# Joined one-hot steps in the expert top-k, and 32 tokens of the second layer on the gathered-row path

## The chip, the core and the metric

The kernel runs on one core of a Trainium2 chip. The metric is the time of one execution on the device in microseconds (us). Engines are named as in the profile: PE is TensorE's matrix multiply and PEld its weight loads, DVE is VectorE, ACT is ScalarE, POOL is GpSimd, SP issues most transfers.

## The reference

The program is a two-layer encoder trunk over 272 tokens (16 learned ones and 256 of the input), model width 1024. Each layer has a token mixer (a recurrent block in layer 0, a convolution module in layer 1) and then an expert layer, the part that matters here:

```python
s1, i1 = lax.top_k(scores[:, :, 0], 16)          # 8 heads, 128 keys on each of two axes
s2, i2 = lax.top_k(scores[:, :, 1], 16)
cand = (s1[..., :, None] + s2[..., None, :]).reshape(c, 8, 256)
s, flat = lax.top_k(cand, 16)
idx1 = jnp.take_along_axis(i1, flat // 16, axis=-1)
idx2 = jnp.take_along_axis(i2, flat % 16, axis=-1)
expert = idx1 * 128 + idx2                       # one of 16384 experts
g = jax.nn.softmax(s, axis=-1)
act = jax.nn.gelu(jnp.einsum('chkd,cd->chk', expert_u[expert], xc))
return jnp.einsum('chk,chkd->cd', g * act, expert_v[expert])
```

Layer 0 computes this for all 272 tokens, layer 1 for 256, since the 16 learned tokens are dropped at the end.

## The kernel before

**Dense path.** For most tokens the kernel doesn't gather experts. It multiplies the tokens with all 16384 rows of U and of V in 128 units each, and masks with the gates. A unit (512 KB) is loaded by SP into `raw`, rounded to fp32r by ACT (`hi`, line 137), and the rest `lo = raw - hi` is made by POOL or DVE (line 144). In U a unit is 24 matmuls: 8 of `hi` with the tokens' high part, 8 of `hi` with their low part, 8 of `lo` with the high part (line 172). Their moving operand has n columns, n the number of dense tokens, 240 in both layers (`LATE[layer][0]`). In V a unit is 8 matmuls of `hi` with both parts side by side (2n = 480 columns, line 632) and 8 of `lo` (240 columns, line 636). Every matmul has its own 128x128 weight load. The last four units of V are split otherwise.

**Top-k and gates.** Ahead of U come the queries (16 units of `w_query`) and the scores (line 522). While the first units of U run on PE, DVE does the top-k of the dense tokens in two tiles of up to 128 partitions (`topk_steps`): per head the best 16 keys of each axis, the 256 sums `cand`, their best 16 (`fi`), and then the key numbers: for each axis the position (`pu`, `pf`) is compared with 0 to 15 (`oh`), multiplied with the axis's key numbers `s16` and added up into `idx`. In this time POOL makes `lo`, two buffers deep; from unit 46 on (`LO_FROM`) DVE makes it, in program order behind all of the top-k. From unit 64 on DVE also builds one-hot gates for 8 tokens at a time, and PE multiplies them (lines 590, 591, 16 matmuls a chunk).

**Gathered-row path.** Groups of 16 tokens (`FEW`), 8 heads each, fill 128 partitions. `few_pick` makes their scores (4 matmul passes) and spreads the token's vector over the heads' rows (16 matmul passes, line 861, with operands that POOL copies, line 859). A top-k of its own gives 16 expert numbers for each row. Then 16 gathers from U by POOL's indirect DMA (line 887) feed 16 dot products on DVE (line 896), and 16 gathers from V feed 16 weighted sums (lines 920, 922); 8 matmuls (16 passes, line 671) add the result to the dense sum. A group in `EARLY` has its top-k ahead of U's unit 46 and 10 of its dot products between units 40 and 63 of U; the rest stands in V. A group in `LATE` has everything in V. Layer 0 has one of each (tokens 256 to 271 early, 240 to 255 late), layer 1 one late group (tokens 240 to 255).

**Order.** The instructions of each engine stand in an order that is fixed when the program is built; `issue_after` ties some of them to others. `few_plan` spreads a layer's gathers, dots and sums evenly over V's units.

Of the kernel before, what the change touches and what calls it, by code (L numbers as in the profile page):

```python
# [17 lines left out]
P = 128  # L18
D = 1024
# [6 lines left out]
NK = 128  # L26
# [5 lines left out]
CC = 8  # L32
HC = 8
FEW = META
EARLY, LATE = ((256,), ()), ((240,), (240,))
DOTS_FROM, DOTS, AHEAD, LO_FROM = 40, 10, 2, 46
JG = 4
JA = 64
# [21 lines left out]
class Trunk:  # L60
# [712 lines left out]
    def topk_steps(self, sp, sc, m, H):  # L773
        nc = self.nc
        K = TOPK
        sv = sp.tile([P, H, 2, K], F32, tag="sv", name="sv", bufs=1)
        si = sp.tile([P, H, 2, K], U32, tag="si", name="si", bufs=1)
        for b in range(2 * H):
            s = sc[:m, b, :]
            v, i = sv[:m, b // 2, b % 2, :], si[:m, b // 2, b % 2, :]  # L780
# [7 lines left out]
        cand = sp.tile([P, H, K, K], F32, tag="cand", name="cand", bufs=1)  # L788
# [3 lines left out]
        fi = sp.tile([P, H, K], U32, tag="fi", name="fi", bufs=1)  # L792
        for h in range(H):
            s = cand[:m, h].rearrange("p a b -> p (a b)")
            v, i = fv[:m, h, :], fi[:m, h, :]
# [4 lines left out]
            nc.vector.max(v[:, 8:16], r[:m])  # L800
            nc.vector.max_index(i[:, 8:16], v[:, 8:16], r[:m])
            yield
        s16 = sp.tile([P, H, 2, K], F16, tag="s16", name="s16", bufs=1)
        nc.vector.tensor_copy(s16[:m], si[:m])
        idx = sp.tile([P, 2, H, K], F32, tag=f"idx{H}", name="idx", bufs=2)
        for ax in range(2):
            pu = sp.tile([P, H, K], U32, tag="pu", name="pu", bufs=1)
            if ax == 0:
                nc.vector.tensor_scalar(pu[:m], fi[:m], 4, None, op0=OP.logical_shift_right)
            else:  # L810
                nc.vector.tensor_scalar(pu[:m], fi[:m], 15, None, op0=OP.bitwise_and)
            pf = sp.tile([P, H, K], F16, tag="pf", name="pf", bufs=1)
            nc.vector.tensor_copy(pf[:m], pu[:m])
            oh = sp.tile([P, H, K, K], F16, tag="oh", name="oh", bufs=1)
            nc.vector.tensor_tensor(oh[:m], self.iota16[:m, None, None, :].to_broadcast([m, H, K, K]),  # L815
                                    pf[:m, :, :, None].to_broadcast([m, H, K, K]), op=OP.is_equal)
            nc.vector.tensor_tensor(oh[:m], oh[:m], s16[:m, :, ax, None, :].to_broadcast([m, H, K, K]), op=OP.mult)  # L817
            nc.vector.tensor_reduce(idx[:m, ax], oh[:m], op=OP.add, axis=AX.X)
            yield
        return idx, fv  # L820

    def softmax(self, sp, fv, m, H=HEADS):
# [17 lines left out]
    def few_pick(self, sp, kp, q, xs, layer, t0):  # L840
# [8 lines left out]
                             start=True, stop=True)  # L849
        sc = (sp if early else kp).tile([P, 2, NK], F32, name=f"sc{t0}", bufs=1)  # L850
        nc.scalar.activation(sc, ps[:, :2], AF.Copy)
        wide = sp.tile([P, D], F32, tag="kept" if early else "rows", name="wide", bufs=1 if early or layer else AHEAD + 1)
        for h in range(2):
            pw = self.bank(5 + h, "wide_ps")
            for lo in range(2):
# [70 lines left out]
    def few_plan(self, vp, kp, early, late, scale, layer, ahead=2):  # L926
        steps = []
        for few in early + late:
            lo = DOTS if few in early else 0
            steps += [lambda few=few: self.few_load(vp, few)]  # L930
            steps += [lambda few=few, lo=lo, k=k: self.few_dot(vp, few, k, lo, TOPK, ahead) for k in range(TOPK - lo + ahead)]
            steps += [lambda few=few: self.few_gelu(few, few is late[-1]), lambda few=few: self.few_weigh(few, scale)]
            steps += [lambda few=few, k=k: self.few_add(vp, few, k, ahead) for k in range(TOPK + ahead)] + [few]
        first = 1 if early else 16
        self.steps = [(first + i * (NK - 4 * JG - first) // len(steps), f) for i, f in enumerate(steps)]
        self.sums = []
        self.picks = [self.few_late(kp, few, layer) for few in late]

# [249 lines left out]
```

## Time and profile before

| | |
|---|---|
| median of 3 executions | 1878.39 us (1878.09 to 1879.69) |
| the profiled execution | 1877.54 us |
| its span, first to last instruction | 1875.7 us, 35733 instructions |
| PE busy | 1809.0 us (96%) |
| PEld busy | 1713.9 us (91%) |
| DVE busy | 1553.2 us (83%) |
| ACT, POOL busy | 943.9 us (50%), 413.8 us (22%) |
| mean granted TensorE clock | 0.990 of 2.4 GHz |

Layer 0's U begins at 189.7 us and its V at 582.6; layer 1's U at 1134.6 and its V at 1514.7. A matmul's duration in the trace holds its passage through the array, so matmuls overlap, and the price of one is the distance from its start to the next one's.

### The profile page before, as it was taken

How to read it: one execution, taken by the hardware profiler on the slowest of the kernel's cores; microseconds unless marked ns; L12 is line 12 of the kernel's file. 1: busy time of each engine (PE TensorE's matmuls, PEld its weight loads, DVE VectorE, ACT ScalarE, POOL GpSimd, SP SyncE). 2: the span in 40 equal slices, each digit the busy share in tenths (PEclk: the TensorE clock that was granted, in tenths of full speed). 3: DMA queues.
4: the chain of work that ended last, by engine and by line, in shares of the span. 5: the costliest groups of instructions: out<-in, count | busy, mean ns of one | idle time of the engine just before them, and what ended most of it. 6: DMA issues, size and time to landing. Idle time of an engine off the chain costs nothing.

```text
span 1875.7 us, 35733 instructions
## 1 busy us (share of the span) xinstructions
PE 1809.0 (96%) x13925; PEld 1713.9 (91%) x13925; DVE 1553.2 (83%) x2793; ACT 943.9 (50%) x1533; POOL 413.8 (22%) x282
## 2 busy tenths in 40 slices
PE   7899998999999999999999999999999999999996
PEld 6789998999998999999899799999999989999995
DVE  8985999889998787777699769996899976776765
ACT  6744543455444444885480545445554445454442
POOL 1111897100001232221000027980000000111200
PEclk9999999999999999999999999999999999999998
DMA  5345566755556898987540355566555567887863
GB/s 200 106 160 167 162 197 181 259 178 161 169 169 231 299 317 274 322 283 267 176 145 25 111 182 162 181 193 196 174 164 168 169 226 233 283 287 254 279 202 112
DMA packets 105337, 376.30 MB, mean 201 GB/s; under 512 B 11600, under 2 KB 12752, under 8 KB 105040
## 3 DMA queue, kind: packets, MB, share of 16 engines
q1 hardware_dynamic: 91344, 323.69, 53.4%
q0 software_dynamic: 13824, 50.34, 8.1%
q8 instruction: 109, 1.79, 0.4%
q14 instruction: 60, 0.49, 0.1%
HBM read 369.20 MB, written 4.78 MB: 199 GB/s over the span
## 4 chain that ended last, share of the span: by engine, by line
PE 78%; DVE 13%; issue 5%; POOL 2%; ACT 1%; DMA 0%; POOLq 0%; SPq 0%; DVEq 0%; ACTq 0%
PE u L172 36%; PE acc L632 22%; PE acc L636 12%; PE cv L1078 2%; PE g L590 1%; PE g L591 1%; DVE lo L144 1%; POOL lo L144 1%; DVE oh L815 1%; DVE oh L817 1%; DVE si L783 1%; DVE r L784 1%; DVE si L786 1%; DVE cand L789 0%; PE sps L522 0%
## 5 line engine op out<-in xcount | busy, mean ns | idle before, releaser
L137 ACT ACTIVATE hi<-raw 128x1024 fp32r<-128x1024 f32 x587 | 620.9, 1059 | 651.9 <-PE u L172 214.7
L144 DVE TENSOR_TENSOR lo<-raw,hi 128x1024 fp32r<-128x1024 f32 x500 | 611.7, 1226 | 216.7 <-PE acc L636 109.6
L172 PE MATMUL u<-xs,hi 128*128 128x240 f32 (+2 forms) x5120 | 656.1, 279 | 15.7 <-ACT xs L206 5.7
L172 PEld LDWEIGHTS u<-xs,hi 128*128 128x128 f32 x5120 | 617.4, 190 | 20.0 <-ACT xs L318 7.1
L632 PE MATMUL acc<-w,hi 128*128 128x480 f32 x1984 | 474.1, 381 | 2.0 <-DVE w L209 2.0
L632 PEld LDWEIGHTS acc<-w,hi 128*128 128x128 f32 x1984 | 354.4, 188 | 47.4 <-DVE w L209 2.4
L172 PE MATMUL u<-xs,lo 128*128 128x240 f32 (+2 forms) x2560 | 357.0, 280 | 16.2 <-DVE lo L144 8.1
L172 PEld LDWEIGHTS u<-xs,lo 128*128 128x128 f32 x2560 | 322.8, 190 | 21.0 <-POOL lo L144 10.5
L636 PEld LDWEIGHTS acc<-w,lo 128*128 128x128 f32 x2048 | 268.0, 189 | 18.2 <-DVE lo L144 3.4
L636 PE MATMUL acc<-w,lo 128*128 128x240 f32 x2048 | 273.4, 275 | 1.3 <-DVE lo L144 1.3
L144 POOL TENSOR_TENSOR lo<-raw,hi 128x1024 fp32r<-128x1024 f32 x92 | 243.2, 2664 | 82.6 <-ACT hi L137 65.0
L887 POOL DMA_INDIRECT rows<-u_rows,ids x48 | 61.8, 1287 | 713.3 <-ACT hi L137 269.9
L887 POOL DMA_INDIRECT rows<-peer_v,ids x48 | 68.9, 1435 | 224.8 <-DVE few_out L922 125.4
L597 ACT ACTIVATE act_b<-g 128x496 f32<-128x496 f32 (+29 forms) x60 | 23.5, 391 | 117.3 <-DVE act_b L560 99.1
L573 DVE TENSOR_TENSOR AB<-iota,iT 128x2048 f16<-128x2048 f16 x60 | 73.0, 1217 | 0.0
L590 PE MATMUL g<-AB 128*128 128x128 f16 x480 | 60.6, 220 | 0.0
L591 PE MATMUL g<-Bl,AB 128*128 128x128 f16 x480 | 60.0, 219 | 0.0
L896 DVE SCALAR_TENSOR_TENSOR rows<-rows,wide 128x1024 f32<-128x1024 f32 x48 | 58.5, 1218 | 0.0
L922 DVE SCALAR_TENSOR_TENSOR few_out<-rows,act,few_out 128x1024 f32<-128x1024 f32 x45 | 57.5, 1279 | 0.0
L316 POOL TENSOR_SCALAR xs<-x,par 128x272 fp32r<-128x272 f32 (+1 forms) x6 | 6.0, 997 | 227.9 <-DVE x L308 165.9
L209 DVE TENSOR_TENSOR w<-act_b,w 128x960 fp32r<-128x960 f32 x32 | 36.9, 1153 | 15.4 <-ACT w L206 15.3
L590 PEld LDWEIGHTS <-AB 128*128 128x128 f16 x480 | 45.4, 97 | 1.9
(256 smaller groups left out, 1713.8 us busy)
## 6 DMA issues: line engine op xcount, KB each, us to landing
raw<-peer_u SPq DMA_DIRECT2D x256, 512.0 KB, 3.9
raw<-peer_v SPq DMA_DIRECT2D x248, 512.0 KB, 4.5
raw<-w_query SPq DMA_DIRECT2D x32, 512.0 KB, 3.6
raw<-pw SPq DMA_DIRECT2D x24, 512.0 KB, 3.6
raw<-w_in SPq DMA_DIRECT2D x16, 512.0 KB, 4.4
raw<-w_out SPq DMA_DIRECT2D x8, 512.0 KB, 4.2
raw<-peer_v SPq DMA_DIRECT2D x16, 256.0 KB, 3.8
wide<-wide SPq DMA_DIRECT2D x6, 512.0 KB, 3.3
```

The lines of the kernel that those rows point to most:

```text
L137: self.act_hi = nc.scalar.activation(hi, raw, AF.Copy).ins
L144: i = e.tensor_tensor(lo[:, s], raw[:, s], hi[:, s].bitcast(F32), op=OP.subtract)
L172: self.mm = nc.tensor.matmul(ps[:, :n], l[:, k, :], xs(k, r)[:, :n], start=start, stop=stop)
L573: nc.vector.tensor_tensor(AB.rearrange("p x c (a b) -> p (x c) a b", b=2), keys, iT[:, c0 // HC].rearrange("p x c b -> p (x c) b")[:, :, N ...
L590: nc.tensor.matmul(ps[:, c, :], A, Bh, start=True, stop=False)
L591: nc.tensor.matmul(ps[:, c, :], A, Bl, start=False, stop=True)
L632: self.mm = nc.tensor.matmul(acc[b][:, :2 * n].rearrange("p (a t) -> p a t", a=2), hi, w[:, :, :n], start=j == 0, stop=j == NK - JG - 1, s ...
L636: self.mm = nc.tensor.matmul(main[b][:, :n], hi if p_ else lo, w[:, i, :n], start=False, stop=j == NK - 1 and not p_, skip_group_check=True)
L887: self.nc.gpsimd.indirect_dma_start(out=t, out_offset=None, in_=table, in_offset=bass.IndirectOffsetOnAxis(ap=few["ids"][:, i, k:k + 1], a ...
L896: self.nc.vector.scalar_tensor_tensor(t, t, 1.0, few["x"], op0=OP.mult, op1=OP.mult, accum_out=few["act"][:, i:i + 1])
L922: nc.vector.scalar_tensor_tensor(few["out"], t, w, few["out"], op0=OP.mult, op1=OP.add)
L1078: self.mm = nc.tensor.matmul(ps[:, :m], diag[i, b, k], h[j][:, s + k:s + k + m], start=(i, j, k) == steps[0], stop=(i, j, k) == steps[-1])
```

## The change

On VectorE, the position, compare and multiply steps of the two axes become one set of instructions over both axes (`s16`, `pu`, `pf`, `oh`, `idx` hold both). `pf` keeps each position twice, so that the compare reads pairs. `oh` takes the buffer of `cand`. In layer 1 tokens 240 to 255 become an early group and tokens 224 to 239 a late one, and n falls from 240 to 224. Layer 0 keeps its groups.

```diff
-EARLY, LATE = ((256,), ()), ((240,), (240,))
+EARLY, LATE = ((256,), (240,)), ((240,), (224,))
...
+        s16 = sp.tile([P, 2, H, K], F16, tag="s16", name="s16", bufs=1)
+        nc.vector.tensor_copy(s16[:m], si[:m].rearrange("p h a k -> p a h k"))
+        pu = sp.tile([P, 2, H * K], U32, tag="pu", name="pu", bufs=1)
+        fp = fi[:m].rearrange("p h k -> p (h k)")
+        nc.vector.tensor_scalar(pu[:m, 0], fp, 4, None, op0=OP.logical_shift_right)
+        nc.vector.tensor_scalar(pu[:m, 1], fp, 15, None, op0=OP.bitwise_and)
+        pf = sp.tile([P, 2 * H * K, 2], F16, tag="pf", name="pf", bufs=1)
+        nc.vector.tensor_copy(pf[:m], pu[:m].rearrange("p a n -> p (a n)")[:, :, None].to_broadcast([m, 2 * H * K, 2]))
+        yield
+        oh = sp.tile([P, 2 * H, K, K], F16, tag="cand", name="oh", bufs=1)
+        pairs = [m, 2 * H * K, K // 2, 2]
+        nc.vector.tensor_tensor(oh[:m].rearrange("p g k (a b) -> p (g k) a b", b=2),
+                                self.iota16[:m].rearrange("p (a b) -> p a b", b=2)[:, None].to_broadcast(pairs),
+                                pf[:m, :, None, :].to_broadcast(pairs), op=OP.is_equal)
+        nc.vector.tensor_tensor(oh[:m], oh[:m],
+                                s16[:m].rearrange("p a h k -> p (a h) k")[:, :, None, :].to_broadcast([m, 2 * H, K, K]),
+                                op=OP.mult)
+        yield
         idx = sp.tile([P, 2, H, K], F32, tag=f"idx{H}", name="idx", bufs=2)
-        for ax in range(2):
-            pu = sp.tile([P, H, K], U32, tag="pu", name="pu", bufs=1)
...
-            nc.vector.tensor_reduce(idx[:m, ax], oh[:m], op=OP.add, axis=AX.X)
-            yield
+        nc.vector.tensor_reduce(idx[:m].rearrange("p a h k -> p (a h) k"), oh[:m], op=OP.add, axis=AX.X)
+        yield
...
-        first = 1 if early else 16
-        self.steps = [(first + i * (NK - 4 * JG - first) // len(steps), f) for i, f in enumerate(steps)]
+        self.steps = [(1 + i * (NK - 4 * JG - 1) // len(steps), f) for i, f in enumerate(steps)]
```

On DVE, at the end of layer 0's top-k (the second tile, 112 tokens), the order before reads:

```order
L809 TENSOR_SCALAR pu<-fi 112x128
L813 CAST pf<-pu 112x128
L815 TENSOR_TENSOR oh<-iota_98,pf 112x2048
L811 TENSOR_SCALAR pu<-fi 112x128
L817 TENSOR_TENSOR oh<-oh,s_2460 112x2048
L813 CAST pf<-pu 112x128
L818 TENSOR_REDUCE idx<-oh 112x128
L815 TENSOR_TENSOR oh<-iota_98,pf 112x2048
L817 TENSOR_TENSOR oh<-oh,s_2460 112x2048
L818 TENSOR_REDUCE idx<-oh 112x128
L896 SCALAR_TENSOR_TENSOR rows,act_2234<-rows,wide 128x1024
L144 TENSOR_TENSOR lo<-raw,hi 128x1024
```

and now:

```order
L807 TENSOR_SCALAR pu<-fi 112x128
L808 TENSOR_SCALAR pu<-fi 112x128
L810 CAST pf<-pu 112x512
L814 TENSOR_TENSOR oh<-iota_98,pf 112x4096
L817 TENSOR_TENSOR oh<-oh,s_2446 112x4096
L822 TENSOR_REDUCE idx<-oh 112x256
L900 SCALAR_TENSOR_TENSOR rows,act_2227<-rows,wide 128x1024
L144 TENSOR_TENSOR lo<-raw,hi 128x1024
```

Ten instructions became six, and the last of them still stands right ahead of the first dot and of unit 46's `lo` (the last two rows).

On PE, between the queries and the first unit of U in layer 1, the rows before were (`sps` are scores, `wide_ps` the spread vectors of a group, `u` in the last row the first unit of U):

```order
L522 MATMUL sps<-sk,q 128x128 x16
L522 MATMUL sps<-sk,q 112x128 x16
L848 MATMUL sps<-sk,q_13737 128x128
L848 MATMUL sps<-sk,q_13740 128x128
L861 MATMUL wide_ps<-eye,xw 128x128 x16
L172 MATMUL u<-xs_12747,hi 128x240 x4
```

and now:

```order
L522 MATMUL sps<-sk,q 128x128 x16
L852 MATMUL sps<-sk,q_13508 128x128
L852 MATMUL sps<-sk,q_13511 128x128
L865 MATMUL wide_ps<-eye,xw 128x128 x16
L522 MATMUL sps<-sk,q 96x128 x16
L852 MATMUL sps<-sk,q_13792 128x128
L852 MATMUL sps<-sk,q_13795 128x128
L865 MATMUL wide_ps<-eye,xw 128x128 x16
L172 MATMUL u<-xs_12719,hi 128x224 x4
```

A second group's scores and spread vectors stand ahead of U, the second tile has 96 tokens instead of 112, and U's matmuls have 224 columns.

On POOL, from the spread vectors' copies (`xw`) to the end of layer 1's gathers, the rows now are (before, one block of 16 copies, 46 `lo`, 16 gathers from U and 16 from V):

```order
L863 CAST xw<-xs_12719 128x128 x8
L144 TENSOR_TENSOR lo<-raw,hi 128x1024 x2
L863 CAST xw<-xs_12720 128x128 x8
L863 CAST xw<-xs_12719 128x128 x8
L863 CAST xw<-xs_12720 128x128 x8
L144 TENSOR_TENSOR lo<-raw,hi 128x1024 x39
L891 DMA rows<-u_rows,ids_13559 128x1024
L144 TENSOR_TENSOR lo<-raw,hi 128x1024 x2
L891 DMA rows<-u_rows,ids_13559 128x1024
L144 TENSOR_TENSOR lo<-raw,hi 128x1024 x2
L891 DMA rows<-u_rows,ids_13559 128x1024
L144 TENSOR_TENSOR lo<-raw,hi 128x1024
```

Three gathers now stand between the last `lo` of POOL; the other 61 of the two groups follow.

## Rows read from the trace of the kernel before

**Rows 1.** The stretches of the two expert layers: U up to unit 46, the rest of U, V; layer 0 first, then layer 1. Columns: stretch, length, busy time and count of PE, PEld, DVE, ACT, POOL, the granted clock, the share of the 16 DMA engines, GB/s.

```profile
189.70:332.80 143.10, 131.70 (x1131) 130.15 (x1132) 142.72 (x374) 64.12 (x96) 121.74 (x49) 0.97 0.60 179
332.80:582.60 249.80, 248.36 (x2431) 246.94 (x2430) 223.55 (x347) 123.05 (x263) 5.57 (x6) 1.00 0.60 189
582.60:920.10 337.50, 336.90 (x2058) 305.72 (x2058) 260.38 (x294) 198.91 (x296) 81.51 (x62) 1.00 0.83 286
1134.60:1266.70 132.10, 129.56 (x1135) 127.87 (x1136) 128.38 (x353) 63.90 (x95) 119.46 (x44) 1.00 0.60 184
1266.70:1514.70 248.00, 247.01 (x2428) 245.84 (x2426) 213.31 (x320) 122.96 (x263) 0.00 (x0) 1.00 0.56 174
1514.70:1848.80 334.10, 334.10 (x2035) 303.44 (x2036) 236.12 (x260) 162.62 (x163) 36.54 (x32) 1.00 0.76 253
```

**Rows 2.** The timeline of PE where U begins and where unit 46 ends, in layer 0 (first four) and layer 1 (last two). Columns: start, length, engine, line, operation, tiles, shapes, count, and in brackets the idle time before it and what ended it.

```profile
189.69 2.02 PE L172 MATMUL u<-xs,hi 128*128 128x240 f32 x16
...
320.18 1.97 PE L172 MATMUL u<-xs,lo 128*128 128x240 f32 x8 [2.32 <-POOL lo L144]
...
330.65 2.06 PE L172 MATMUL u<-xs,lo 128*128 128x240 f32 x8 [5.89 <-DVE lo L144]
332.51 1.76 PE L172 MATMUL u<-xs,hi 128*128 128x240 f32 x8
...
1134.65 2.02 PE L172 MATMUL u<-xs,hi 128*128 128x240 f32 x16
...
1266.12 1.96 PE L172 MATMUL u<-xs,hi 128*128 128x240 f32 x16
```

**Rows 3.** The timeline of DVE at the end of layer 0's top-k (second tile), down to unit 46's `lo`.

```profile
308.69 0.22 DVE L809 TENSOR_SCALAR pu<-fi 112x128 uint32<-112x128 uint32 x1
...
309.21 7.45 DVE L815 TENSOR_TENSOR oh<-iota,pf 112x2048 f16<-112x2048 f16 x1
...
322.44 2.29 DVE L815 TENSOR_TENSOR oh<-iota,pf 112x2048 f16<-112x2048 f16 x1
324.77 1.23 DVE L817 TENSOR_TENSOR oh<-oh,s 112x2048 f16<-112x2048 f16 x1
...
329.37 1.22 DVE L144 TENSOR_TENSOR lo<-raw,hi 128x1024 fp32r<-128x1024 f32 x1
```

**Rows 4.** The same steps of layer 0's first tile on DVE's timeline, beside a steadily working POOL, and the end of layer 1's top-k.

```profile
217.72 1.94 DVE L809 TENSOR_SCALAR pu<-fi 128x128 uint32<-128x128 uint32 x1
...
220.19 4.23 DVE L815 TENSOR_TENSOR oh<-iota,pf 128x2048 f16<-128x2048 f16 x1
...
226.70 3.43 DVE L817 TENSOR_TENSOR oh<-oh,s 128x2048 f16<-128x2048 f16 x1
...
242.75 2.27 DVE L818 TENSOR_REDUCE idx<-oh 128x128 f32<-128x2048 f16 x1
...
1257.48 2.29 DVE L818 TENSOR_REDUCE idx<-oh 112x128 f32<-112x2048 f16 x1
1261.11 2.01 DVE L144 TENSOR_TENSOR lo<-raw,hi 128x1024 fp32r<-128x1024 f32 x1 [1.34 <-ACT hi L137]
```

**Rows 5.** From the page, the costliest groups: a compare that reads pairs (the gates' one-hot), and a group's weighted sum on DVE. Columns: line, engine, operation, out<-in, shapes, count | busy us, mean ns of one | idle before.

```profile
L573 DVE TENSOR_TENSOR AB<-iota,iT 128x2048 f16<-128x2048 f16 x60 | 73.0, 1217 | 0.0
...
L922 DVE SCALAR_TENSOR_TENSOR few_out<-rows,act,few_out 128x1024 f32<-128x1024 f32 x45 | 57.5, 1279 | 0.0
```

**Rows 6.** The timeline of POOL in layer 0: a `lo` beside DVE's steps that search a maximum, and the first gather's issue.

```profile
286.68 2.39 POOL L144 TENSOR_TENSOR lo<-raw,hi 128x1024 fp32r<-128x1024 f32 x1 [0.29 <-PE u L172]
...
302.67 1.14 POOL L887 DMA_INDIRECT rows<-u_rows,ids  x1 [2.06 <-DVE fv L797]
```

**Rows 7.** The timelines of PE and PEld, by which the distance from one matmul to the next is read for moving operands of 128, 256, 240, 16 (weight loads), and 480 and 240 columns.

```profile
175.84 3.79 PE L522 MATMUL sps<-sk,q 128*128 128x128 f32 x32
179.46 0.67 PE L848 MATMUL sps<-sk,q 128*128 128x128 f32 x4
...
1121.24 2.05 PE L172 MATMUL u<-xs,hi 128*128 128x256 f32 x16
...
1124.08 7.43 PE L522 MATMUL sps<-sk,q 128*128 128x128 f32 x64
...
1263.43 1.95 PE L172 MATMUL u<-xs,hi 128*128 128x240 f32 x16
...
1700.15 1.90 PE L632 MATMUL acc<-w,hi 128*128 128x480 f32 x8
1701.89 1.06 PE L636 MATMUL acc<-w,lo 128*128 128x240 f32 x8
1702.78 1.93 PE L632 MATMUL acc<-w,hi 128*128 128x480 f32 x8
...
1816.35 1.86 PEld L671 LDWEIGHTS acc<-same,few_out 128*128 128x128 f32 x16
1818.13 0.96 PEld L632 LDWEIGHTS acc<-w,hi 128*128 128x128 f32 x5
```

**Rows 8.** PE's timeline: a group's scores ahead of U in layer 0 (its spread vectors follow, up to 189.69), and in layer 1 the first matmul of one gate chunk and the first of the unit behind it.

```profile
186.37 0.69 PE L848 MATMUL sps<-sk,q 128*128 128x128 f32 x4
...
1324.18 0.23 PE L590 MATMUL g<-AB 128*128 128x128 f16 x1
...
1325.06 2.04 PE L172 MATMUL u<-xs,hi 128*128 128x240 f32 x16
```

More of the change, by code (lines that the diff above doesn't have):

```diff
@@ L802, in topk_steps @@
             yield
-        s16 = sp.tile([P, H, 2, K], F16, tag="s16", name="s16", bufs=1)
-        nc.vector.tensor_copy(s16[:m], si[:m])
-        idx = sp.tile([P, 2, H, K], F32, tag=f"idx{H}", name="idx", bufs=2)
-        for ax in range(2):
-            pu = sp.tile([P, H, K], U32, tag="pu", name="pu", bufs=1)
[L808 to L817, printed above, removed]
-            nc.vector.tensor_reduce(idx[:m, ax], oh[:m], op=OP.add, axis=AX.X)
-            yield
+        s16 = sp.tile([P, 2, H, K], F16, tag="s16", name="s16", bufs=1)
@@ L851, in few_pick @@
         nc.scalar.activation(sc, ps[:, :2], AF.Copy)
-        wide = sp.tile([P, D], F32, tag="kept" if early else "rows", name="wide", bufs=1 if early or layer else AHEAD + 1)
+        wide = sp.tile([P, D], F32, tag="kept" if early else "rows", name="wide", bufs=1 if early else AHEAD + 1)
         for h in range(2):
```

## The prediction

> **What bounds the kernel.** I read the table by stretches first [rows 1]. PE is busy in nearly all of each stretch, 336.9 of 337.5 us in layer 0's V, 334.1 of 334.1 in layer 1's, at a granted clock of 1.00, so there the price of a matmul counts. One stretch differs: layer 0's U up to unit 46 takes 143.1 us with PE busy 131.7, while DVE is busy 142.7. The timeline of PE shows why [rows 2]: it waits 2.32 us for a POOL `lo` and then 5.89 us for unit 46's `lo`, which DVE makes. From U's first matmul to the end of unit 46 are 332.51 - 189.69 = 142.8 us in layer 0 and 1266.12 - 1134.65 = 131.5 in layer 1, for the same 47 units: 11.3 more. The timeline of DVE [rows 3] shows the one-hot steps right ahead of that `lo`: DVE makes it at 329.37 because the top-k isn't done earlier. In layer 1, whose top-k has no third group, DVE's last top-k step ends at 1259.77, and `lo` then waits 1.34 us for ACT [rows 4]. So DVE bounds layer 0 for a short while, nearly bounds layer 1, and elsewhere PE does.
>
> **The change, PE's part.** Distances from start to start [rows 7]: 24 matmuls of 256 columns in 1124.08 - 1121.24 = 2.84 us, 118.3 ns each; 24 of 240 columns in 1266.12 - 1263.43 = 2.69, 112.1 each; 32 of 128 columns in 179.46 - 175.84 = 3.62, 113.1 each; and 16 weight loads for matmuls of 16 columns in 1818.13 - 1816.35 = 1.78, 111.3 each. So the distance falls with the columns down to 240 and not below: some 111 ns is the price of a 128x128 fp32 weight load, and 240 columns stand at that corner. In V, 8 matmuls of 480 columns take 1.74 us, 217.5 each, and 8 of 240 take 0.89, 111.3 each [rows 7].
>
> *V's wide matmuls.* 124 units of 8, so 992, go from 480 to 448 columns. By proportion they cost 203.0; by the slope between 240 and 480 columns, 106.2 / 240 = 0.44 ns a column, 203.3. Neither is near the corner. I take 13.9 ns each, -13.8 us (13 to 14.5).
>
> *The narrow ones.* 128 x 24 in U, 128 x 8 in V and 64 in V's last four units, 4160, go from 240 to 224. At the corner nothing is saved; if the step from 256 to 240 (6.2 ns) went on, 25.8 us. I take the nearest rows, those of 16 and 128 columns: 0.8 ns each, -3.3 us.
>
> *Gates.* n / 8 falls from 30 chunks to 28; one takes 1325.06 - 1324.18 = 0.88 us [rows 8]: -1.8.
>
> *The second group of layer 1.* Its scores and spread vectors stand on PE ahead of U, where nothing covers them; a group took 189.69 - 186.37 = 3.3 us in layer 0 [rows 2, 8]: +3.3. Its 16 passes in V take 16 x 111 ns [rows 7]: +1.8.
>
> **The change, DVE's part.** A two-input step is slower beside a working POOL: the 2048-element compare took 4.23 us in the first tile and 2.29 alone, the multiply 3.43 and 1.23 [rows 3, 4]. So each such step waits about 2 us for one `lo` of POOL (2.39 us, [rows 6]), and fewer steps wait less often. The joined compare has 4096 elements; the trace shows none like it. From below, it reads pairs as the gates' compare does, 1217 ns for 2048 [rows 5], so about 2.3 us; from above, as the old compare, 4.5. I take 2.3, by the row whose operands are built alike. First tile before: 217.72 to 245.02, 27.3 us. After: two `pu` 2.1, `pf` 2.4, compare and multiply 2.3 + 2.0 each, reduce 4.4, the maximum searches between them about 1.5: 19. It saves 8. The second tile took 308.69 to 328.3, 19.6 [rows 3]; with two waits it takes about 13.5 and saves 6. The group in between saves some 4 (three waits fewer, of 2 us each, less what its short steps don't wait). In all 18 us before unit 46 in layer 0, where PE waited 8.2: DVE is no longer last.
>
> What is late next is POOL. It begins a `lo` 0.3 us behind PE's release and takes 2.39; PE wants it after 16 of the next unit's 24 matmuls, so it has about 2.0 us to spare, and regains 0.3 a unit. Three gathers of 1.14 [rows 6] take 3.4 of that, which the spare nearly covers, but the joined steps take turns with it. Layer 1's lateness without a third group is the nearest row; it also holds two tiles' conflicts, which shrink by about a third. So layer 0 falls from 142.8 to about 131.8: -11 us (-3 if POOL takes most of the place, -13 if its own lateness shrinks too).
>
> A rule speaks against the joining. The Trainium skill (SBUF — State Buffer, "Who interferes with whom") says that a Vector instruction with two SBUF inputs and a GpSimd instruction that reads SBUF exclude each other for the whole instruction. The rows on the compare (4.23 against 2.29) agree. By it a joined step of 2.3 us would hold POOL longer than its 2.0 us to spare, two of them in turn about 2 us per tile; the sum by the rule would be 2 to 4 us higher, inside the range.
>
> *Layer 1's U.* Its DVE gets the third group. Layer 0's top-k ended 328.3 - 189.7 = 138.6 us behind U's start, layer 1's 125.1, and U begins 3.3 later now: the group adds about 17, and the joining takes off 4 + 8 + 8. So it ends about 3 us earlier than now, at 1257, where `lo` is wanted at about 1264: covered, with 7 us to spare. It inherits the gathers on POOL and 10 dots behind unit 46; layer 0's later stretch is 249.8 - 248.0 = 1.8 longer [rows 1]. With the shorter one-hot against that I take +1.5 (from -2 to the 11.3 of layer 0).
>
> *Layer 1's V.* DVE gets 6 dots and 16 sums more, 22 x 1.28 = 28 us [rows 5], on 236.1 of 334.1 [rows 1]; layer 0's V carries that load (260.4 of 337.5, DMA share 0.83 against 0.76) and is 3.4 us longer, of which 1.8 are counted above. +1.5, from 0 to 4, since a unit is now 0.11 us shorter. The late group's top-k, spread over V's first units, gets shorter beside an idle POOL: nothing.
>
> **Sum.** -13.8 - 3.3 - 1.8 + 3.3 + 1.8 - 11 + 1.5 + 1.5 = -21.8. The profiled execution took 1877.54, so 1855.7; the median is 0.85 above it, so about 1856.5. I say 1856, by itself 1847 to 1866.
>
> **Rivals.**
>
> *The columns pay in full.* Then the narrow matmuls give 25.8 instead of 3.3: 1834. For it, 256 to 240 still fell by 6.2 ns; against it, 16 and 128 columns cost no less than 240. The Trainium skill (TensorE: Matmul & The Clock Gate, "Back-to-back issue gap") gives N / 2.4 + 2.5 ns for a matmul by itself, 95.8 at 224 columns against 102.5, which would be this case; "LDWEIGHTS" there gives columns / 1.2, so 107 ns for 128 whatever the moving size, and the 111.3 of the 16-column rows agrees with that.
>
> *DVE stays the bound.* If the joined compare runs at one element a cycle (4.5 us) or its waits grow with its length, half the saving is left: layer 0 gains 4 and layer 1 loses 5, and the sum is about -11: 1867. If nothing is saved, layer 0 keeps its time and layer 1, with its third group, gets layer 0's 11.3: -13.8 - 3.3 - 1.8 + 5.1 + 11.3 + 1.8 + 1.5 = +0.8: 1879, no change. For it, DVE is busy in all of both stretches; against it, the pairs of rows 5.
>
> *Slower: layer 1's V turns to DVE.* If gathers land late, a dot or sum that waits holds the `lo` queued behind it on DVE, and PE starves. If the 28 us of new steps lay open, the sum would be +6: 1884. It decides once DVE's share nears the whole: (236 + 28 - 2) / 321 = 82% is expected, 77% is what layer 0 runs at without idling PE, so it needs waits of another 50 us.
>
> **How the numbers follow.** The forecast 0.70; the columns in full 0.08; DVE with half the saving 0.12, with none 0.05; V on DVE 0.03; and 0.02 for what I don't see. The range 1844 to 1869 takes in the half-saving case and leaves out the others. A measurement here can tell 0.2%, 3.8 us, from no change: faster 0.91 (the first three, and a little), same 0.05, slower 0.04.
>
> **What would show it.** V's wide matmuls about 203 ns apart; U's narrow ones still about 111 apart (near 104 if the columns pay); no wait of PE for DVE's `lo` at unit 46 in either layer; layer 0's U up to unit 46 near 132 us; the joined compare 2.3 us alone and near 4.3 beside POOL; PE busy in all of layer 1's V. A gap of PE ahead of unit 46, or `lo` behind late gathers in V, would prove me wrong.

## The result, and the profile after

The changed kernel takes 1857.81 us (median of 4 runs, 1855.10 to 1859.18) against 1878.95 (1878.09 to 1879.69): ratio 0.9887, 95% interval 0.9872 to 0.9903. The forecast was 1856. The profiled execution took 1857.75 us with a span of 1856.0, 19.7 less than the span before. This total agrees better than its parts do. (One execution of the last experiment took 3627 us, which nothing here explains; the ratios leave it out.) From the starts of the stretches' first matmuls:

| stretch | before | after | moved | forecast |
|---|---|---|---|---|
| up to U of layer 0 | 189.69 | 190.94 | +1.25 | 0 |
| U of layer 0, to the end of unit 46 | 142.8 | 136.1 | -6.7 | -11 |
| the rest of that U | 250.1 | 249.4 | -0.7 | 0 |
| V of layer 0 | 337.5 | 336.5 | -1.0 | 0 |
| from there to U of layer 1 (second group's pick) | 214.55 | 217.60 | +3.05 | +3.3 |
| U of layer 1 | 380.0 | 380.0 | 0.0 | -2.8 |
| V of layer 1 | 334.2 | 322.9 | -11.3 | -11.4 |
| behind V, to the end of the span | 26.9 | 22.5 | -4.3 | 0 |

Two of them are off by 4.3 us in opposite directions: layer 0's U gave less than forecast, and the end of the kernel gave what nothing in the forecast provides for. The 1.25 us ahead of layer 0's U is scatter: this start lay between 189.4 and 191.7 in the executions below.

The page's head and its chain of waits:

```profile
PE 1793.9 (97%) x13929; PEld 1714.4 (92%) x13929; DVE 1562.6 (84%) x2849; ACT 940.7 (51%) x1537; POOL 484.6 (26%) x330
...
PE 81%; DVE 7%; issue 6%; POOL 3%; DMA 2%; ACT 1%; POOLq 0%; SPq 0%; DVEq 0%; ACTq 0%
```

DVE had 13% of this chain and has 7%; DMA had 0% and has 2%. The same stretches as in [rows 1], in the same order and columns:

```profile
190.90:327.10 136.20, 130.03 (x1130) 128.75 (x1131) 125.56 (x362) 63.20 (x94) 123.58 (x49) 0.99 0.60 188
327.10:576.40 249.30, 247.92 (x2432) 246.54 (x2430) 223.47 (x346) 123.99 (x263) 5.08 (x6) 1.00 0.60 189
576.40:912.90 336.50, 336.46 (x2057) 306.06 (x2058) 259.21 (x290) 199.05 (x296) 81.44 (x62) 1.00 0.83 287
1130.50:1264.00 133.50, 128.81 (x1128) 127.92 (x1129) 131.64 (x362) 62.48 (x94) 123.14 (x49) 0.99 0.61 191
1264.00:1510.60 246.60, 245.18 (x2403) 244.09 (x2401) 216.51 (x335) 122.20 (x261) 5.33 (x6) 1.00 0.60 191
1510.60:1833.50 322.90, 319.98 (x2052) 304.37 (x2052) 254.41 (x285) 159.57 (x164) 93.24 (x54) 1.00 0.86 299
```

Read the first line: DVE's busy time fell from 142.7 to 125.6 us, by 17, close to the 18 forecast. PE's idle time in the stretch didn't go with it. Who made PE wait there, before (first fence, layer 0 and then layer 1) and after (second); columns: waiting engine and tile, what it waited for, us in all, times, longest:

```profile
PE u L172 <- DVE lo L144: 5.9, 1, 5.9
PE u L172 <- POOL lo L144: 5.5, 5, 2.3
...
PE u L172 <- POOL lo L144: 2.4, 5, 0.8
```

```profile
PE u L172 <- POOL lo L144: 6.2, 6, 2.6
...
PE u L172 <- POOL lo L144: 4.6, 3, 2.8
```

The wait for DVE is gone, and the waits for POOL are longer, in layer 1 too. First DVE's own timeline, the joined steps of tile 1 and of tile 2 in layer 0, `lo` of unit 46, and the joined compare of layer 1's second tile [rows 3, 4]:

```profile
218.97 1.93 DVE L807 TENSOR_SCALAR pu<-fi 128x128 uint32<-128x128 uint32 x1
...
221.76 4.21 DVE L814 TENSOR_TENSOR oh<-iota,pf 128x4096 f16<-128x4096 f16 x1
226.10 4.27 DVE L817 TENSOR_TENSOR oh<-oh,s 128x4096 f16<-128x4096 f16 x1
230.57 4.39 DVE L822 TENSOR_REDUCE idx<-oh 128x256 f32<-128x4096 f16 x1
...
301.51 2.29 DVE L814 TENSOR_TENSOR oh<-iota,pf 112x4096 f16<-112x4096 f16 x1
303.84 2.29 DVE L817 TENSOR_TENSOR oh<-oh,s 112x4096 f16<-112x4096 f16 x1
306.16 4.42 DVE L822 TENSOR_REDUCE idx<-oh 112x256 f32<-112x4096 f16 x1
...
321.56 2.84 DVE L144 TENSOR_TENSOR lo<-raw,hi 128x1024 fp32r<-128x1024 f32 x1 [9.84 <-PE u L172]
...
1241.15 7.17 DVE L814 TENSOR_TENSOR oh<-iota,pf 96x4096 f16<-96x4096 f16 x1
```

4096 elements in 2.29 us, as long as 2048 took in the old form [rows 3]; 4.2 beside POOL, and 7.17 in layer 1's second tile, where two `lo`s of POOL stood back to back (4.73 us). Tile 1's steps take 234.96 - 218.97 = 16.0 us instead of 27.3, tile 2's 310.58 - 298.58 = 12.0 instead of 19.6. DVE then sits idle for 9.84 us ahead of unit 46. It has more room than it needs.

PE in the same place, and POOL beside it:

```profile
308.38 2.06 PE L172 MATMUL u<-xs,lo 128*128 128x240 f32 x8 [2.63 <-POOL lo L144]
...
313.98 1.16 PE L172 MATMUL u<-xs,lo 128*128 128x240 f32 x8 [1.14 <-POOL lo L144]
...
317.50 1.17 PE L172 MATMUL u<-xs,lo 128*128 128x240 f32 x8 [0.57 <-POOL lo L144]
...
323.36 0.83 PE L172 MATMUL u<-xs,lo 128*128 128x240 f32 x5 [0.22 <-POOL lo L144]
```

```profile
298.80 2.39 POOL L144 TENSOR_TENSOR lo<-raw,hi 128x1024 fp32r<-128x1024 f32 x1 [0.30 <-PE u L172]
303.45 1.36 POOL L891 DMA_INDIRECT rows<-u_rows,ids  x1 [2.26 <-PE u L172]
304.85 9.08 POOL L144 TENSOR_TENSOR lo<-raw,hi 128x1024 fp32r<-128x1024 f32 x2
314.08 0.95 POOL L891 DMA_INDIRECT rows<-u_rows,ids  x1 [0.15 <-issue]
315.06 4.72 POOL L144 TENSOR_TENSOR lo<-raw,hi 128x1024 fp32r<-128x1024 f32 x2
```

POOL's `lo` ends at 301.19. The next instruction is a gather. It starts at 303.45, 2.26 us later and 0.35 before DVE's compare ends at 303.80 (the releaser in brackets, PE, is inferred; the `lo`s start 0.3 us behind theirs). Such a pause stood ahead of the first gather before the change too, 2.06 us long while DVE searched maxima [rows 6], so the joined compare need not be its cause; what POOL waits for there isn't shown. The `lo` behind the gather is put beside DVE's multiply. Two `lo`s then take 9.08 us instead of 4.8, the second of them alone

```profile
308.29 5.64 POOL L144 TENSOR_TENSOR lo<-raw,hi 128x1024 fp32r<-128x1024 f32 x1
```

and it ends 2.2 us behind DVE's first dot (310.50 to 311.72). From there POOL works without a pause and needs until 323 to catch up. Whether the gathers with their dots or the joined steps are to blame can't be read here; the experiments part them.

V of layer 1, the distances on PE's timeline [rows 7]:

```profile
1694.90 1.78 PE L632 MATMUL acc<-w,hi 128*128 128x448 f32 x8
1696.51 1.04 PE L636 MATMUL acc<-w,lo 128*128 128x224 f32 x8
1697.40 1.78 PE L632 MATMUL acc<-w,hi 128*128 128x448 f32 x8
```

8 wide matmuls of 448 columns take 1.61 us, 201.3 ns each (217.5 before); 8 narrow ones of 224 take 0.89, 111.3, as before. But PE now waits in this V, where it had not waited for `lo` once. ACT's wait ahead of such a place names the transfer of V's weights, and behind ACT's late `hi` stand ACT's `w` (the rounded activations) and DVE's `w`, both ahead of the `lo` that PE wants (the lines are of PE's waits and of the timelines of ACT and DVE):

```profile
PE acc L636 <- DVE lo L144: 2.9, 4, 1.2
...
1555.12 1.06 ACT L137 ACTIVATE hi<-raw 128x1024 fp32r<-128x1024 f32 x1 [3.03 <-DMA raw<-peer_v]
...
1557.05 1.09 DVE L209 TENSOR_TENSOR w<-act_a,w 128x896 fp32r<-128x896 f32 x1 [3.71 <-ACT w L206]
```

ACT's waits for these weights in the whole of layer 1's V, before (first fence) and after:

```profile
ACT hi L137 <- DMA raw<-peer_v: 24.1, 14, 3.3
```

```profile
ACT hi L137 <- DMA raw<-peer_v: 94.0, 59, 4.5
```

The end of the kernel, the drain of POOL's queue behind its last instruction, before and after (columns: line, queue, operation, count: shortest/median/longest ns, first and last start):

```profile
L1184 POOLq DRAIN  x3: 45/102/10630, 1864.3 to 1875.4; - x3
```

```profile
L1187 POOLq DRAIN  x3: 45/102/4585, 1848.9 to 1855.7; - x3
```

10.63 us before and 4.59 after, while no engine is busy. Before, it ended last; after, SyncE does, which waits for the output's transfers until 1855.1, so of the 6.04 us the span gets 4.3. No line of the diff touches that place.

### The profile page after: what moved, and what is told of

It reads as the page before. It is cut to its first block, busy times and chain, and to the rows that moved or that the text cites. A ratio compares the mean times of both kernels' runs of the same rounds, so it can differ in the third digit from the quotient of the medians.

```text
span 1856.0 us, 35898 instructions
## 1 busy us (share of the span) xinstructions
PE 1793.9 (97%) x13929; PEld 1714.4 (92%) x13929; DVE 1562.6 (84%) x2849; ACT 940.7 (51%) x1537; POOL 484.6 (26%) x330
## 3 DMA queue, kind: packets, MB, share of 16 engines
q8 instruction: 109, 1.79, 0.4%
## 4 chain that ended last, share of the span: by engine, by line
PE 81%; DVE 7%; issue 6%; POOL 3%; DMA 2%; ACT 1%; POOLq 0%; SPq 0%; DVEq 0%; ACTq 0%
PE u L172 42%; PE acc L632 20%; PE acc L636 11%; POOL lo L144 2%; PE cv L1081 2%; DVE lo L144 2%; DMA raw<-peer_v 2%; PE g L590 1%; PE g L591 1%; PE sps L522 1%; PE wide_ps L865 1%; DVE rows L900 0%; PE acc L671 0%; POOL rows L891 0%; ACT t L385 0%
## 5 line engine op out<-in xcount | busy, mean ns | idle before, releaser
L172 PE MATMUL u<-xs,hi 128*128 128x224 f32 (+3 forms) x5120 | 656.0, 279 | 15.6 <-ACT xs L206 6.4
L632 PE MATMUL acc<-w,hi 128*128 128x480 f32 (+1 forms) x1984 | 458.5, 373 | 2.0 <-DVE w L209 2.0
L172 PE MATMUL u<-xs,lo 128*128 128x240 f32 (+3 forms) x2560 | 355.7, 279 | 13.6 <-POOL lo L144 10.7
L636 PE MATMUL acc<-w,lo 128*128 128x240 f32 (+1 forms) x2048 | 272.1, 274 | 3.7 <-DVE lo L144 3.6
L891 POOL DMA_INDIRECT rows<-u_rows,ids x64 | 94.5, 1476 | 638.4 <-DVE sv L782 450.0
L891 POOL DMA_INDIRECT rows<-peer_v,ids x64 | 104.9, 1638 | 226.1 <-DVE few_out L926 118.6
L597 ACT ACTIVATE act_b<-g 128x368 f32<-128x368 f32 (+43 forms) x58 | 22.6, 390 | 113.4 <-DVE act_b L560 95.2
L900 DVE SCALAR_TENSOR_TENSOR rows<-rows,wide 128x1024 f32<-128x1024 f32 x64 | 78.9, 1233 | 0.6 <-DMA rows<-u_rows,ids 0.6
L209 DVE TENSOR_TENSOR w<-act_b,w 128x960 fp32r<-128x960 f32 (+1 forms) x32 | 35.9, 1123 | 22.1 <-ACT w L206 21.8
L209 DVE TENSOR_TENSOR w<-act_a,w 128x960 fp32r<-128x960 f32 (+3 forms) x38 | 36.3, 969 | 18.2 <-ACT w L206 18.1
```

The source lines that it names most:

```text
L172: self.mm = nc.tensor.matmul(ps[:, :n], l[:, k, :], xs(k, r)[:, :n], start=start, stop=stop)
L209: nc.vector.tensor_tensor(lo, src, hi.bitcast(F32), op=OP.subtract)
L632: self.mm = nc.tensor.matmul(acc[b][:, :2 * n].rearrange("p (a t) -> p a t", a=2), hi, w[:, :, :n], start=j == 0, stop=j == NK - JG - 1, s ...
L636: self.mm = nc.tensor.matmul(main[b][:, :n], hi if p_ else lo, w[:, i, :n], start=False, stop=j == NK - 1 and not p_, skip_group_check=True)
L891: self.nc.gpsimd.indirect_dma_start(out=t, out_offset=None, in_=table, in_offset=bass.IndirectOffsetOnAxis(ap=few["ids"][:, i, k:k + 1], a ...
L900: self.nc.vector.scalar_tensor_tensor(t, t, 1.0, few["x"], op0=OP.mult, op1=OP.mult, accum_out=few["act"][:, i:i + 1])
```

## The experiments

There are eleven runs, one of them of the kernel before. Ratios are to the kernel before, timed on the same chip in the same job. There it took 1878.2 to 1880.0 us, so a difference between kernels of two jobs is good to about 2 us.

**The joined one-hot alone.** The changed kernel with before's groups, and with the two lines that hang on them (the buffers of `wide`, the first step of V) as they were:

```diff
-EARLY, LATE = ((256,), (240,)), ((240,), (224,))
+EARLY, LATE = ((256,), ()), ((240,), (240,))
...
```

> The joined one-hot alone, with before's token groups. Theory A (DVE's top-k ended last ahead of unit 46 in layer 0, and POOL takes part of its place): layer 0's U up to the end of unit 46 falls from 142.8 to about 136 us, as in the changed kernel, layer 1's (which has no third group here) falls by 1 to 2 of its 131.5, nothing else moves: about -8 us, 1870. Rival B (the gain in layer 0 came from the 240 instead of 256... columns of other parts, not from the one-hot): 0. Rival C (without the gathers' group in layer 1, DVE's joined steps hold POOL as long as they save): layer 1 gets slower by 2 to 3, about -4.

1869.65 us, ratio 0.9951 (0.9938 to 0.9965). Layer 0's U up to unit 46 took 136.3 us, layer 1's 131.0. That is theory A, with 0.5 us in layer 1 in place of 1 to 2. PE waited 6.4 us for POOL in layer 0, as in the changed kernel, and none for DVE. POOL's last drain took 10.63 us.

**The two groups alone.** The kernel before with the new groups and the same two lines, its per-axis one-hot kept:

```diff
-EARLY, LATE = ((256,), ()), ((240,), (240,))
+EARLY, LATE = ((256,), (240,)), ((240,), (224,))
...
```

> The two groups in layer 1 alone, with before's per-axis one-hot. Theory A (the two parts need each other: with the old one-hot the third group makes layer 1's DVE late): V of layer 1 -11 us, the pick ahead of its U +3, its U up to unit 46 later by 6 to 11 (layer 0 with a third group took 11.3 more than layer 1 without one), the rest -1 to -2: between -4 and +2, about 1877. Rival B (layer 1's top-k has the room, since its U starts 3 us later): U of layer 1 0 to +2, sum about -9, 1870.

1876.68 us, ratio 0.9990 (0.9981 to 0.9999). Layer 1's U up to unit 46 took 142.0 instead of 131.5 us. Its PE timeline at unit 46:

```profile
1266.40 1.95 PE L172 MATMUL u<-xs,hi 128*128 128x224 f32 x16
1279.34 2.05 PE L172 MATMUL u<-xs,lo 128*128 128x224 f32 x8 [10.99 <-DVE lo L144]
```

So what V gains is paid for by a DVE that is 11 us late. The end of the kernel gave its 4.3 us here too (the drain took 4.58); without it the groups alone would have cost some 2 us. The parts alone give 9.2 and 2.2 us, together 11.4; the changed kernel gives 21.1. Some 8 of the 9.7 us between them are this wait: layer 1's U up to unit 46 takes 142.0 us with the old one-hot, 133.7 with the joined one.

**Half the columns in U's `lo` matmuls.**

```diff
-            self.mm = nc.tensor.matmul(ps[:, :n], l[:, k, :], xs(k, r)[:, :n], ...)
+            w = 128 if n < 256 and i == 1 else n
+            self.mm = nc.tensor.matmul(ps[:, :w], l[:, k, :], xs(k, r)[:, :w], ...)
```

> The changed kernel with the lo matmuls of U in both layers on 128 columns in place of 240 and 224 (it leaves out that part of the weights' low product for the tokens behind the first 128). 1024 matmuls lose 104 columns on average. Theory A (a matmul of 240 columns and fewer costs its weight load, 111 to 112 ns): the 1024 distances stay within 1 ns, the time within 2 us of the changed kernel. Rival B (columns pay, 0.44 ns each as between 240 and 480): 1024 x 104 x 0.44 = 47 us less, 1811. Rival C (half way: the 256 to 240 step's 6 ns goes on a little): 3 to 8 us less.

1855.99 us, ratio 0.9876 (0.9861 to 0.9891): no change within the measurement. Its PE timeline in layer 1, a unit of 16 matmuls with 224 columns and 8 with 128:

```profile
1132.84 1.99 PE L173 MATMUL u<-xs,hi 128*128 128x224 f32 x16
1134.67 1.01 PE L173 MATMUL u<-xs,lo 128*128 128x128 f32 x8
1135.52 1.99 PE L173 MATMUL u<-xs,hi 128*128 128x224 f32 x16
```

The unit takes 2.68 us, and so it does in the changed kernel. The 8 short ones take 0.85 us instead of 0.89, and the 16 beside them 1.83 instead of 1.79. The edit touches 2048 matmuls, 8 in each of 256 units, and not 1024 as the expectation has it, so rival B's price is 94 us. All of U in both layers got 2.5 us shorter, 1.2 ns for each of them. Columns below 240 cost next to nothing; the rival in which they pay is dead.

**The kernel before, profiled again.** No edit.

> The kernel before, profiled a second time, to see how far two executions differ where no code differs. Theory A (the 4.3 us that the changed kernel's span is shorter behind the issue of the output's transfers, and the 1.25 us by which layer 0's U started later, belong to the execution): from the last matmuls' end to the span's end somewhere between 22 and 27 us here, U of layer 0 starting between 189 and 191. Rival B (they belong to the change): 26.9 and 189.7 again, to within 0.3.

U of layer 0 began at 190.30, and its part up to unit 46 took 143.4. The drain took 10.63 us again and the stretch behind the last matmul into the accumulators 17.77 us, against 17.76 in the first profile and 13.44 in the changed kernel. So the start is scatter, and the end is not.

**U's gathers behind POOL's last `lo`.**

```diff
-DOTS_FROM, DOTS, AHEAD, LO_FROM = 40, 10, 2, 46
+DOTS_FROM, DOTS, AHEAD, LO_FROM = 46, 7, 2, 46
```

> The changed kernel with U's gathers and dots begun at unit 46 instead of 40 (7 instead of 10 dots in U, 3 more in V), so that no gather stands between POOL's lo's. PE waited 2.63 + 1.14 + 0.57 + 0.22 us for POOL's lo in layer 0's units 40 to 46 and 2.77 + 0.38 in layer 1's. Theory A (the gathers that stand between the lo's make POOL late): these waits fall to 2 or less in each layer, 136.1 to about 133 in layer 0 and 133.7 to about 132 in layer 1; V gets 3 dots more, 0 to +2: -2 to -4 in all. Rival B (the joined steps' hold on the port makes POOL late, the gathers only wait with it): the first wait stays over 2 us in both layers, the sum moves by less than 1.5.

1850.40 us, ratio 0.9838 (0.9825 to 0.9852): faster than the changed kernel by 7.4 us (9 by the ratios), more than theory A had said. U up to unit 46 took 131.3 us in layer 0 and 130.3 in layer 1. PE's waits there:

```profile
PE u L172 <- POOL lo L144: 3.4, 4, 1.4
...
PE u L172 <- POOL lo L144: 2.9, 2, 1.4
```

6.2 and 4.6 us became 3.4 and 2.9. What is left is mostly two waits of 1.4 us a layer, one per tile, where a joined step and a `lo` meet. The edit moves the gathers and their dots together, so the gain is that of both. V of layer 1, with three dots more, took 322.7 us: covered.

**DVE makes U's `lo` earlier.**

```diff
-... lambda j: FULL if j >= LO_FROM else (("p", 1024),), u_store)
+... lambda j: FULL if j >= (45 if layer else 43) else (("p", 1024),), u_store)
```

> The changed kernel with DVE making U's lo from unit 43 in layer 0 and 45 in layer 1, instead of 46 in both. Theory A (DVE is done with the top-k well before, idle 9.8 us in layer 0, and POOL is what PE waits for): the waits at units 43 to 46 of layer 0, 1.14 + 0.57 + 0.22, and the 0.38 of layer 1 go, the first one of each layer stays: U of layer 0 up to unit 46 from 136.1 to about 134.3, about -2 in all. Rival B (DVE comes late for unit 43, behind the reduce and the dots): a wait for DVE in their place, 0 to +3.

1853.30 us, ratio 0.9860 (0.9845 to 0.9875). Layer 0 took 133.5 us and layer 1 132.9, 3.4 us less together. The waits that stand at the units which POOL no longer serves are gone, and the first one stays at 2.6 and 2.8. DVE had the room, and POOL was the bound. In layer 0 DVE's `lo` of unit 43 now stands ahead of the first dot, and the `lo` of POOL that had taken 5.64 us takes 2.37. So the dot, and not only the gathers, seems to have held POOL up; no run moves it alone.

**The joined steps cut in two.**

```diff
-        nc.vector.tensor_tensor(oh[:m]..., op=OP.is_equal)
-        nc.vector.tensor_tensor(oh[:m], oh[:m], s16..., op=OP.mult)
+        for ax in range(2):
+            o = oh[:m, ax * H:ax * H + H]
+            nc.vector.tensor_tensor(o..., op=OP.is_equal)
+        for ax in range(2):
+            o = oh[:m, ax * H:ax * H + H]
+            nc.vector.tensor_tensor(o, o, s16[:m, ax]..., op=OP.mult)
```

> The changed kernel with the joined compare and the joined multiply cut in two by axis, pairs kept, so four DVE steps of 1.2 us in place of two of 2.3. Theory A (POOL is late because one step holds the port for 2.3 us): the first PE wait of units 40 to 46 falls from 2.6 and 2.8 us to 1.5, U up to unit 46 by 1 to 2 in each layer. Rival B (each two-input step takes one turn with a lo of 2.4 us, however short it is): tile 1's four steps take about 4 x 3.3 in place of 2 x 4.2 us, DVE's top-k gets 4 us longer a tile, PE's waits for POOL stay or grow: 0 to +3.

1863.83 us, ratio 0.9911 (0.9895 to 0.9926), 6 us slower than the changed kernel (4.5 by the ratios), more than rival B allowed. DVE's timeline of tiles 1 and 2 in layer 0, and PE's waits of that stretch:

```profile
223.35 6.64 DVE L816 TENSOR_TENSOR oh<-iota,pf 128x2048 f16<-128x2048 f16 x2
229.91 6.75 DVE L821 TENSOR_TENSOR oh<-oh,s 128x2048 f16<-128x2048 f16 x2
...
307.75 7.18 DVE L816 TENSOR_TENSOR oh<-iota,pf 112x2048 f16<-112x2048 f16 x2
314.86 4.53 DVE L821 TENSOR_TENSOR oh<-oh,s 112x2048 f16<-112x2048 f16 x2
```

```profile
PE u L172 <- DVE lo L144: 6.0, 1, 6.0
PE u L172 <- POOL lo L144: 2.5, 5, 1.2
```

In tile 1, beside a POOL that works steadily in both kernels, the same elements take 13.4 us in four steps and 8.5 in two (4.21 and 4.27): 3.3 us a step, as rival B said. In tile 2 they take 11.7 and 4.6, but there POOL stood at a gather in the changed kernel, and its two steps met no `lo`. PE's waits for POOL did get shorter (1.2 at most), but DVE now takes more turns with `lo`, and PE waits 6.0 us for DVE at unit 46 in both layers. This is what the join of these two steps buys: not less arithmetic but fewer turns. It isn't the larger part of the one-hot's gain. This kernel, with pairs and the other steps joined, is already 12.9 us faster than the groups with the old one-hot; the joined compare and multiply add the 6.0.

**Half of V's gathered rows.**

```diff
-        if k < TOPK:
+        if k % 2 and k < TOPK:
+            few["rows"][k] = few["rows"][k - 1]
+        elif k < TOPK:
             few["rows"][k] = self.few_rows(vp, few, self.a["peer_v"]..., 1, k, ahead + 1)
```

> The changed kernel with every second gather of V's rows left out in both layers, the row before used in its place (so half of the rows of V that a group sums are wrong ones); DVE's sums stay as many. The gathers fall from 128 to 96. Theory A (PE's four waits in layer 1's V, 0.63 + 1.27 + 0.90 + 1.58 us of distance, come from weights that land late beside the gathers): they go, V of layer 1 falls from 322.9 to about 319. Rival B (they come from dots and sums queued ahead of lo on DVE): they stay. On the end of the kernel: if the number of gathers sets how long POOL's last drain lasts (10.6 us in the runs with 96 gathers, 4.6 in those with 128), it lasts 10.6 here and the tail is 4.3 us longer; if the second token group or its code sets it, it stays 4.6. So A with the drain by the number is about 0 in all, A without it -4.

1860.87 us, ratio 0.9894 (0.9879 to 0.9909). PE's waits for `lo` in V of layer 1 fell from 2.9 us to 1.2, those at 48 and 109 us behind its start went, and those at 9 and 161 stayed, where U's rows are gathered. But V took as long as in the changed kernel, 323.1 us: the wide matmuls that were 201 ns apart were 205 apart from 40 us behind V's start on, in the same program but for the gathers. So theory A's 4 us in V didn't come. The end of the kernel answered to the number of gathers, the groups being those of the changed kernel: with 96 left, the drain took 10.63 us.

**Half of U's rows in V's stretch as well.** The same edit, and in the function that issues a dot:

```diff
+        if nxt < hi == TOPK and nxt % 2:
+            few["rows"][nxt] = few["rows"][nxt - 1]
-        if nxt < hi:
+        elif nxt < hi:
             few["rows"][nxt] = self.few_rows(pool, few, self.a["u_rows"], 0, nxt, ahead + 1)
```

> As with the half of V's rows left out, and every second gather of U's rows in V's stretch too (its dots then read the product that the dot before left in the tile). 74 gathers are left. Halving V's rows took away the waits of layer 1's V at 48 and 109 us behind its start and left those at 9 and 161, where U's rows are gathered. Theory A (late weights beside gathers): the one at 161 goes too or falls under 0.6 us. Rival B (DVE's order): it stays at 1.2 to 1.6. On V as a whole: if the two levels of the wide matmuls' distance (201 and 205 ns) give back what the waits took, it stays at 332; if not, it falls to 329 or less. POOL's last drain by the number of gathers: 74 is below 96, so 10 us or more.

1856.62 us, ratio 0.9883 (0.9867 to 0.9898). The window of V in layer 1, and PE's waits in it:

```profile
1511.40:1830.50 319.10, 318.76 (x2052) 304.57 (x2052) 255.48 (x285) 160.58 (x164) 43.83 (x27) 1.00 0.79 258
```

```profile
PE acc L636 <- DVE lo L144: 0.3, 1, 0.3
```

With the DMA share at 0.79 instead of 0.86 three of the four waits are gone, the one of 0.3 us at 9 us behind V's start is left, and V is 3.8 us shorter (the 332 and 329 of the expectation are slips; V had taken 323), DVE's busy time being the same (255.5 against 254.4). ACT's waits for V's weights fell from 94.0 to 64.0 us. So three of the waits came from late weights beside the gathers, not from DVE's order; at all three places of the changed kernel DVE idles (3.7, 2.8 and 3.4 us) until ACT's `w`, which stands behind a late `hi`. The first one is open.

**Three quarters of V's rows.**

```diff
-        if k < TOPK:
+        if k % 4 == 3:
+            few["rows"][k] = few["rows"][k - 1]
+        elif k < TOPK:
```

> The changed kernel with every fourth gather of V's rows left out, so 112 in place of 128 (the sums use the row before in its place). A look at POOL's last drain, 10.63 us in the runs with 96 and 4.58 in those with 128. If it falls evenly with the number: 7.6 us. If there is a step between the two: 10.6 or 4.6. The time else as the changed kernel's, within 2 us.

A single run took 1862.88 us, 5 us above the changed kernel; from the last matmul to the end it is 5.6 us longer. The drain, here and (second fence) with 74 gathers:

```profile
L1189 POOLq DRAIN  x3: 45/102/11935, 1848.3 to 1860.7; - x3
```

```profile
L1191 POOLq DRAIN  x3: 45/102/8833, 1845.9 to 1855.2; - x3
```

Neither of the two expectations holds: it gets longer with the number, and then falls. 74, 96 and 112 gathers give 8.83, 10.63 and 11.94 us, 82 ns a gather in both steps; 128 give 4.58.

**The late gathers in the kernel before.** The same line as for U's gathers above (46, 7), on the kernel before.

> The kernel before with U's gathers and dots begun at unit 46 instead of 40, the edit that took 7 us off the changed kernel. Only layer 0 has gathers in U there. Theory A (DVE bounded it before, POOL bounds it now): PE waits for DVE's lo at unit 46 as before, since the gathers hold up DVE's two-input steps little: 0 to -2 us. Rival B (the gathers on POOL were what made it late before as well): layer 0's U up to unit 46 falls from 143 to 139 or less, -4 or more.

1875.41 us, ratio 0.9983 (0.9974 to 0.9993). Layer 0's U up to unit 46 took 138.6 instead of 142.8 to 143.4 us, by its size rival B; the whole gained 2.8 us, between the two. But what PE waits for is DVE, once and long:

```profile
326.23 2.06 PE L172 MATMUL u<-xs,lo 128*128 128x240 f32 x8 [8.56 <-DVE lo L144]
```

Theory A had the right engine and a wrong price: PE's waits for POOL fell from 5.5 to 1.1 us, and PE resumes at 326.23 in place of 330.65 [rows 2], 4.2 us sooner from U's start. DVE's top-k ends 3.0 us sooner from there, since POOL is done with its `lo`s 6.8 us sooner and DVE's last steps meet none; the rest is the first dot, which no longer stands ahead of DVE's `lo`. So the gathers and dots cost some 4 us in layer 0 before the change as well, by holding up both engines.

## Why the forecast came out, and where its steps didn't

**The total.** 1856 was forecast and 1857.8 measured, well inside the own range of 1847 to 1866. It owes this in part to luck: a gain mis-sized by 4.3 us and an unforeseen one of the same size cancel.

**Layer 0's U: the step that was mis-sized.** "DVE is no longer last" held. The wait of 5.89 us is gone, the joined compare took 2.29 us alone and 4.21 beside POOL, and the top-k ended 119.6 us behind U's start instead of 138.6, 19 sooner for 18 forecast. "What is late next is POOL", too, was right, but the price was not: the term was -11 and measured -6.7. I had set POOL's 2.0 us to spare against three gathers at 1.14 and left the turns with the joined steps in the remainder. The runs give the size: without the gathers and dots between the `lo`s 131.3 us, so 4.8 were theirs; and 131.3 is what the forecast of 131.8 had asked for. The first gather doesn't cost POOL its 1.14 us only. POOL pauses 2.26 us ahead of it; the row that gave the 1.14 shows such a pause, 2.06 us [rows 6], and the prediction left it out. The `lo` behind the gather then takes 3.5 us and the next one, in whose time the first dot falls, 5.64. A gap of PE ahead of unit 46 was named as a sign of being wrong; it came, with POOL in DVE's place.

**The rule on turns.** The Trainium skill (SBUF — State Buffer, "Who interferes with whom") says that the ports which Vector and GpSimd share are an exclusive lock, so that of two instructions that contend for them the first to issue makes the other wait. The runs agree: beside a working POOL four steps in place of two took 13.4 us instead of 8.5 for the same elements. By that rule I had allowed 2 to 4 us more in all. Where only the joined steps meet `lo`, two waits of 1.4 us a layer are left. But such waits stood there before the change too (2.4 us in layer 1, each shorter than 0.9), and without gathers layer 0 took 131.3 us, no more than was forecast without the rule. So the turns are there, and the 2 to 4 us more are not seen.

**Layer 1's U.** +1.5 less 1.8 for the gates and 2.5 for the narrow matmuls was forecast, -2.8, and it came to 0.0. Up to unit 46 it got 2.2 longer, and that is PE's waits for POOL, 4.6 us instead of 2.4: layer 1 inherited the gathers, as the text said, and their price from layer 0. The top-k itself was covered: DVE came 1.3 us ahead of need, less than the 7 that I had worked out; its last compare took 7.17 us, and the first dot, which the working had left out, 2.2. The narrow matmuls gave 0.01 us a unit, 0.4 ns each at most, half of the 0.8 that I took.

**Layer 1's V.** -11.4 against -11.3, but of other parts. The wide matmuls gave 217.5 - 201.3 = 16.2 ns each, about 16 us in place of 13.8; both proportion and slope had been too small. The waits took it back: 2.9 us for `lo`. The text bounded the cost by 0 to 4 and named the share of DMA, 0.83 in layer 0; layer 1 came to 0.86 at 299 GB/s, and that was enough for late weights. "PE busy in all of layer 1's V" was wrong, and the sign named for it, `lo` late in V, came, behind late weights in the place of late gathers. The rival in which V turns to DVE didn't begin: DVE was busy 254 of 323 us, 79%.

**The second group's pick.** +3.05 for +3.3, on PE ahead of U, as read from layer 0.

**The parts and their tie.** The case in which nothing is saved was put at 1879, with layer 1 getting layer 0's 11.3 us. The run of the groups with the old one-hot is that case: layer 1's U 10.5 us longer, 1876.7 us, or 1881 without the shorter drain.

**The end.** 4.3 us came off behind the last transfer's issue. Nothing in the profile before announced it, and only a second profile of a kernel with the same number of gathers told it from scatter.

## What to carry to other kernels

Where two engines take turns at something, count the turns, not the work: joining two steps of VectorE paid because beside a busy GpSimd each step, long or short, waits for one instruction of it, at times two. When a bound is lifted, price the next one by what shares its queue, since that is what gets in its way, and try to move that work first: here one line of constants, which put the gathers and their dots behind the last `lo`, was worth a third of the change again, and with it the kernel takes 1850.4 us. And compare the end of the trace, where no engine is busy, as carefully as its stages.

## What the runs showed of the hardware

*The last drain of POOL's queue depends on how many gathers went before.* 74, 96, 112 and 128 gathers gave 8.83, 10.63, 11.94 and 4.58 us. The first three lie on a line of 82 ns a gather; 128 lies 8.7 us under that line (11.94 + 16 x 0.082 = 13.25). With 96 it was the same to 5 ns in programs that differ in their one-hot and groups, and with 128 to 3 ns, whenever the last gather was. A count that starts over between 112 and 128 would fit; what is counted wasn't tried.

*The wide matmuls of V have two paces.* Of the same program's matmuls with 448 columns most came 201 ns apart in some stretches and 205 in others, at a granted clock of 1.00 in both. In the run with half of V's rows the slower pace held from 40 us behind V's start on and took back what fewer waits gave; in the one with three quarters it held from 200 us on. What sets it is open.

*A weight load's pace is kept over groups.* With 128 columns in 8 of a unit's 24 matmuls, those came 106 ns apart and the 16 others 114, in place of 111 and 112, and the unit stayed at 2.68 us.
